# A hybrid encoder in float32: the SwiGLU's first projection cut into column sets of 512 and 384, and its weight sums built up in place

## Chip, cores and metric

The kernel runs on one core of one Trainium2 chip. The metric is the device time of one execution in microseconds (us); of several runs the median counts, and less is better.

## What is computed

Two layers work on an activation x of 512 tokens by 1024 features, all in float32. A layer is a SwiGLU block, a token mixer (pooling, differential attention, a gated linear recurrence, and their merge) and a second SwiGLU block. One RMSNorm ends the program. So there are four SwiGLU blocks, called FFN 1 to FFN 4 here, each with D_FF = 2816:

```python
def swiglu(h, w_in, w_out):
    gate, up = jnp.split(h @ w_in, 2, axis=-1)
    return (jax.nn.silu(gate) * up) @ w_out

    for l in range(DEPTH):
        lam_init = 0.8 - 0.6 * math.exp(-0.3 * l)
        x = x + 0.5 * swiglu(rms_norm(x, ffn1_norm[l]), ffn1_w_in[l], ffn1_w_out[l])
        x = x + token_mixer(rms_norm(x, mix_norm[l]), ...)
        x = x + 0.5 * swiglu(rms_norm(x, ffn2_norm[l]), ffn2_w_in[l], ffn2_w_out[l])
    return rms_norm(x, final_norm)
```

The change touches the four SwiGLU blocks only; the mixer's arithmetic stays.

## The kernel before

**Precision.** TensorE reads float32 in a rounded form, so each operand is split in two. ACT copies a raw weight into the rounded form, `wh<-raw`, and DVE takes the rest, `wl<-raw,wh`. Three matmuls (high by high, high by low, low by high) make one product. The activations are split the same way (`zh`, `zl` for the first projection, `ah`, `al` for the second).

**Seven products.** Both projections of an FFN cut the matrices into 2 by 2 blocks and use seven block products in place of eight (`seven`, L406). In the code's names they are P1 = A11·W00, P2 = A12·W10, Q5 = S1·(W00+W01), Q3 = S4·W11, P6 = S2·(W00+W01+W11), P7 = S3·(W11+W01) and Q4 = A22·(sum of all four). The S are sums of activation blocks. The sums of weights are made in SBUF by transfers: a load (`load_fn`, L362) goes out on SP's queue, and a transfer that adds on landing (`add_fn`, L365) on POOL's queue. P1, Q5, P6 and Q4 share one raw block, `b1`, to which one matrix is added between two products. Q3 and P7 share `b2` if `chain2` is true, which it is for the first projection. In the second, P7 has a block of its own, which it loads and adds to at once:

```python
                if p == "P1":
                    block = b1[n] = Block([ld(0, 0)])
                    acc = ap(0, 1)
...
                elif p == "Q3":
                    block = b2[n] = Block([ld(1, 1)])
                    acc = ap(0, 1) if chain2 else None
                else:
                    block = b2[n] if chain2 else Block([ld(0, 1)], ap(1, 1))
```

**Units.** The work of all four FFNs and both mixers is one list of units. A unit is one weight tile of 128 partitions by up to 1024 elements with its matmuls. In the first projection the 2816 columns of gate and up are cut into sets (`quad`, L460): five of 512 columns, where a product is two units, and one of 256, where all four row chunks of a product fit into one unit. A set is 7 products of 24 matmuls. In the second projection, the output projection, a product has 11 row chunks, thus 66 matmuls in six units, in the order P1, P2, Q5, Q3, P6, P7, Q4. FFN 1 begins with P1; the other three begin their first set with P2 and then P1.

**What sets the order.** The program is written out unit by unit. `loads` (L1387) issues the loads of coming blocks in advance, as long as no more raw blocks are alive than the limit of the unit just finished (`held`: 8 in the first projection, 10 in the second, set at L1440 in `gap`, L1431). `splits_to` (L1424) makes the high parts three units ahead; `split_hi` (L1398) and its `low` (L1412) make the two parts, and behind the low part the block gets its next addition, or is given back and new loads leave. `gap` runs once per unit, and `defer` puts a step some gaps later.

**Pools.** SBUF holds 20 slots of 2 KB per partition (`SLOTS`, L45; for `u`, `v`, `th` and others) and 40 buffers of 4 KB (`BIGS`, L46; for raw blocks, split weights, activations). `two` (L128) gives two halves of one large buffer.

**Around the products.** What a product leaves in PSUM is copied by ACT (`copies` L480, in the second projection L643) or combined by DVE (`c11_` L498, `p6` L534, `q4` L553; `tanh` L493 for the gate). Twice in a set the gated values `v` and `q5` are transposed by TensorE (`transposes` L465, tile `ht`) and copied into `h`. `rsqrt_newton` (L192) and `inv_rms_start` (L199) belong to the norms.

Of the kernel before, what the change touches and what calls it, by code (L numbers as in the profile page):

```python
# [10 lines left out]
AF = mybir.ActivationFunctionType  # L11
# [6 lines left out]
S = 512  # L18
# [23 lines left out]
C_ID, C_ONE, C_DIST, C_EDGE, C_INVW, C_EPS = 0, 128, 256, 256 + 896, 256 + 896 + 32, 256 + 896 + 34  # L42
NCST = C_EPS + 2

SLOTS = 20  # L45
BIGS = 40  # L46
AHEAD = 6.0
LAG = 2
SCFIRST = False
# [57 lines left out]
def trunk_kernel(ctx, tc, xn, pm, fin, cst, bd, f1i, f1o, win, wbp, wba, wbl, wout, f2i, f2o, out):  # L107
# [10 lines left out]
    def slot(dt=F32, name="s"):  # L118
        return sp.tile([128, S], dt, tag="s", name=name)

    def big(dt=F32, name="b"):
        return bp.tile([128, 2 * S], dt, tag="b", name=name)
# [5 lines left out]
    def two(name="t"):  # L128
        return list(pair(F32, name))
# [58 lines left out]
    def defer(n, fn):  # L188

        tasks.setdefault(clock["gap"] + n, []).append(fn)  # L190

    def rsqrt_newton(y0, m):  # L192
        t, r = slot(name="nt"), slot(name="r")
        V.tensor_tensor(out=t, in0=y0, in1=y0, op=MUL)
        V.scalar_tensor_tensor(out=t, in0=t, scalar=-0.5, in1=m, op0=MUL, op1=MUL)
        V.scalar_tensor_tensor(out=r, in0=t, scalar=1.5, in1=y0, op0=ADD, op1=MUL)
        return r

    def inv_rms_start(acc, n, eps, col):  # L199

        ps = bank("nrm")
        PE.matmul(ps, lhsT=ones, rhs=acc, start=True, stop=True)
        y0, m = slot(name="y0"), slot(name="m")
        A.t += 2.6
        A.activation(out=y0, in_=ps, func=AF.Abs_reciprocal_sqrt, scale=1.0 / n, bias=cs[:, C_EPS + col:C_EPS + col + 1])
        V.tensor_scalar(out=m, in0=ps, scalar1=1.0 / n, scalar2=eps, op0=MUL, op1=ADD)
        return y0, m
# [167 lines left out]
    def flat(n=2 * S):  # L375
        return [(0, lambda raw: raw[:, 0:n], 0, (n,))]
# [26 lines left out]

    LEFT = {"P1": "A11", "P2": "A12", "Q5": "S1", "Q3": "S4", "P6": "S2", "P7": "S3", "Q4": "A22"}

    def seven(order, nk, width, left, wap, after, chain2, held, prep=None):  # L406

        upc = 2 * S // width  # L410
        parts = [(k, min(k + upc, nk)) for k in range(0, nk, upc)]
        b1, b2, box = {}, {}, {}
        for p in order:
            name = LEFT[p]
            for n, (k0, k1) in enumerate(parts):
                ld = lambda r, c, k0=k0, k1=k1: load_fn(wap(r, c, k0, k1), k1 - k0, width)
                ap = lambda r, c, k0=k0, k1=k1: add_fn(wap(r, c, k0, k1), k1 - k0, width)
                acc = None
                if p == "P1":
                    block = b1[n] = Block([ld(0, 0)])  # L420
                    acc = ap(0, 1)
                elif p == "Q5":
                    block, acc = b1[n], ap(1, 1)
                elif p == "P6":
                    block, acc = b1[n], ap(1, 0)
                elif p == "Q4":
                    block = b1[n]
                elif p == "P2":
                    block = Block([ld(1, 0)])
                elif p == "Q3":  # L430
                    block = b2[n] = Block([ld(1, 1)])
                    acc = ap(0, 1) if chain2 else None
                else:
                    block = b2[n] if chain2 else Block([ld(0, 1)], ap(1, 1))

                def mm(u, a0, a1, p=p, name=name, k0=k0, k1=k1):
                    if k0 == 0:
                        box[p] = [bank(p), bank(p)]
                    for tt in range(2):
                        acc_ = box[p][tt][:, 0:width]  # L440
                        for k in range(k0, k1):
                            ah, al = (a[:, tt * 128:tt * 128 + 128] for a in left(name, k))
                            wh, wl = (a[:, (k - k0) * width:(k - k0 + 1) * width] for a in (u.hi, u.lo))
                            PE.matmul(acc_, lhsT=ah, rhs=wh, start=k == 0, stop=False)
                            PE.matmul(acc_, lhsT=ah, rhs=wl, start=False, stop=False)
                            PE.matmul(acc_, lhsT=al, rhs=wh, start=False, stop=k == nk - 1)

                def fin(p=p, last=k1 == nk):
                    if last:
                        after[p](box.pop(p))  # L450

                if prep:
                    prep(p, n, len(units))
                units.append(Unit(block, flat((k1 - k0) * width), mm, fin, acc=acc, held=held, nk=k1 - k0))


    def ffn(wi, wo, done, order0):
        H = {}

        def quad(j, order):  # L460
            w = min(S, DFF - j * S)
            u, c11, q5, v, th0, th1 = {}, {}, {}, {}, {}, {}
            held = {}

            def transposes(hh, src):  # L465
                def fn():
                    for kk in range(2):
                        ps = bank("ht")
                        for i in range(w // 256):
                            for tt in range(2):  # L470
                                c = 2 * i + kk
                                PE.transpose(ps[:, i * 256 + tt * 128:i * 256 + tt * 128 + 128], src[tt][:, c * 128:c * 128 + 128], ident)
                        if (hh, kk, j // 2) not in H:
                            H[hh, kk, j // 2] = big(name="h")
                        o = j % 2 * 512
                        defer(1, lambda kk=kk, ps=ps, o=o: A.activation(out=H[hh, kk, j // 2][:, o:o + w], in_=ps[:, 0:w], func=AF.Copy))
                    src.clear()
                return fn

            def copies(dst):  # L480
                def fn(ps):
                    for tt in range(2):
                        dst[tt] = slot(name="u")
                        A.activation(out=dst[tt][:, 0:w], in_=ps[tt][:, 0:w], func=AF.Copy)
                return fn

# [4 lines left out]
                V.scalar_tensor_tensor(out=out_[:, 0:w], in0=a[:, 0:w], scalar=s, in1=b[:, 0:w], op0=op, op1=MUL)  # L491

            def tanh(th, src, t0):  # L493
                for tt in range(2):
                    th[tt] = slot(name="th")
                    A.activation(out=th[tt][:, 0:w], in_=src[tt][:, 0:w], func=AF.Tanh, scale=st["r"][t0 + tt][1])

            def c11_(ps):  # L498
# [27 lines left out]

            def q3(ps):
                def rest():
                    for tt in range(2):
                        v[tt] = slot(name="v")  # L530
                        add(v[tt], ps[tt], q5[tt])
                later.append(rest)

            def p6(ps):  # L534
                def rest():
                    for tt in range(2):
                        add(u[tt], ps[tt], u[tt])
                        add(v[tt], v[tt], u[tt], SUB)
                        mul(v[tt], v[tt], st["r"][tt][2], th0[tt])
                    th0.clear()  # L540

                later.append(rest)
                defer(2, transposes(0, v))

            def p7(ps):
                def rest():
# [6 lines left out]
            def q4(ps):  # L553
                def rest():
                    for tt in range(2):
                        add(u[tt], ps[tt], u[tt])

                def gate():
                    tanh(th1, u, 2)

                    def h1():
                        for tt in range(2):
                            mul(th1[tt], th1[tt], 1.0, u[tt], ADD)
                            mul(q5[tt], q5[tt], st["r"][2 + tt][2], th1[tt])
                        u.clear()
                        th1.clear()
                    later.append(h1)

                later.append(rest)
                defer(1, gate)  # L570
                defer(3, transposes(1, q5))

            def wap(r, c, k0, k1):
                o = c * DFF + j * S
                return wi[r * 512 + k0 * 128:r * 512 + k1 * 128, o:o + w].rearrange("(k p) f -> p k f", p=128)

            seven(order, 4, w, lambda name, k: [a[:, k * 256:k * 256 + 256] for a in zc[name]], wap,
                  {"P1": p1, "P2": p2, "Q5": copies(q5), "Q3": q3, "P6": p6, "P7": p7, "Q4": q4}, True, 8)

        n0 = len(units)  # L580
        later_order = ["P1", "P2", "Q5", "Q3", "P6", "P7", "Q4"]
        for j in range(6):
            quad(j, order0 if j == 0 else later_order)
        nz = len(units) - 1
        add_hook(nz, zc.clear)

# [55 lines left out]

        def copies(dst):  # L643
            def fn(ps):
                for tt in range(2):
                    dst[tt] = slot(name="u")
                    A.activation(out=dst[tt], in_=ps[tt], func=AF.Copy)
            return fn

# [37 lines left out]
        def left(name, k):  # L687
            return [a[:, k % 4 * 256:k % 4 * 256 + 256] for a in comb[name, k // 4]]

        seven(later_order, KF // 2, S, left, wap,  # L690
              {"P1": o_p1, "P2": o_p2, "Q5": o_q5, "Q3": o_q3, "P6": o_p6, "P7": o_p7, "Q4": o_q4}, False, 10, prep)


    def mixer(l, side, done, between):
# [867 lines left out]
```

## Time and profile before

| | |
|---|---|
| runs, us | 2223.81, 2219.13, 2217.24 |
| median, us | 2219.13 |
| profiled execution: its own time, us | 2214.34 |
| its span between first and last record, us | 2212.2 |
| mean granted TensorE clock | 0.985 |
| busy: TensorE (PE), DVE, ACT, POOL | 2106.6 (95%), 1656.1 (75%), 1186.4 (54%), 325.7 us (15%) |
| moved by DMA | 322.98 MB, mean 146 GB/s |

The profile is one execution, recorded in hardware. The table's shares are means over stages with different limits: the output projections move weights fastest, the mixers hardly use POOL's queue. TensorE's records overlap, since matmuls are pipelined, so the time of a stage is read from its window and from the distance between the starts of matmuls, and idle time from the waits. All engine operations carry line 83, the helper that issues them, so tiles tell them apart: `P` and `Q` are PSUM tiles of the products, `raw` a loaded block, `ht` a transpose. L366 is the adding transfer. A clock of 1.00 means the higher of TensorE's two levels all the time.

### The profile page before, as it was taken

Reading aid. Unit: us, or ns where it says so; the run is one execution under the profiler, and the core shown is the slowest. Engines: PE = TensorE matmul, PEld = TensorE weight load, DVE = VectorE, ACT = ScalarE, POOL = GpSimd, SP = SyncE. Lnnn points to the kernel's source line nnn. Section 1 sums busy time; section 2 is a strip of 40 time slices with the busy share of each in tenths; the row PEclk is TensorE's granted clock in tenths of the full one; section 3 lists DMA queues with packets and bytes.
Section 4 is the critical chain, followed back from the end, with each engine's and each line's share of the span. In section 5 each row is a group of like instructions: output and inputs, shape, how many; then the busy total and the mean of one; then the engine's idle time right before and its main releaser. Section 6 shows DMA issues by size and latency. Waiting matters only on the chain.

```text
span 2212.2 us, 25981 instructions
## 1 busy us (share of the span) xinstructions
PE 2106.6 (95%) x9640; PEld 1723.0 (78%) x9640; DVE 1656.1 (75%) x2327; ACT 1186.4 (54%) x1735; POOL 325.7 (15%) x276
## 2 busy tenths in 40 slices
PE   7999898999999999989899999989999999999897
PEld 5888786788787777878777888877887877778786
DVE  6877796598777577769777777966967766777697
ACT  7454464645554554546565545646456535555464
POOL 1122230000000021212212211300000001122131
PEclk9999999999999999999999999999999999999999
DMA  9789697123125287878967878951222344779795
GB/s 250 161 163 194 147 210 202 58 65 98 57 86 156 55 182 178 162 158 198 234 135 153 183 183 181 202 167 47 87 67 67 122 126 97 169 156 188 156 209 129
DMA packets 198030, 322.98 MB, mean 146 GB/s; under 512 B 10384, under 2 KB 72336, under 8 KB 197904
## 3 DMA queue, kind: packets, MB, share of 16 engines
q0 software_dynamic: 76032, 138.43, 36.9%
q1 hardware_dynamic: 121872, 182.90, 25.4%
q8 instruction: 75, 1.23, 0.2%
q14 instruction: 51, 0.42, 0.1%
HBM read 319.19 MB, written 2.10 MB: 145 GB/s over the span
## 4 chain that ended last, share of the span: by engine, by line
PE 52%; DMA 21%; DVE 12%; issue 8%; ACT 6%; POOL 2%; SPq 0%; POOLq 0%; ACTq 0%; DVEq 0%
PE ps L83 17%; PE P L83 11%; DMA raw<-in_f1i_dram 9%; PE Q L83 9%; DMA raw<-in_f2i_dram 7%; DVE wl L83 6%; PE o L83 4%; PE y L83 4%; ACT wh L83 3%; DMA raw<-in_f1o_dram 2%; POOL raw L366 2%; PE v L83 1%; PE sc L83 1%; DMA raw<-in_f2o_dram 1%; PE av L83 1%
## 5 line engine op out<-in xcount | busy, mean ns | idle before, releaser
L83 DVE TENSOR_TENSOR wl<-raw,wh 128x1024 fp32r<-128x1024 f32 (+1 forms) x668 | 705.4, 1076 | 294.3 <-ACT wh L83 291.1
L83 ACT ACTIVATE wh<-raw 128x1024 fp32r<-128x1024 f32 (+1 forms) x668 | 606.5, 936 | 380.8 <-DMA raw<-in_f2i_dram 166.9
L83 PE MATMUL ps<-z,wh 128*128 128x512 f32 x1216 | 380.2, 393 | 0.0
L83 PE MATMUL P<-wl,zh 128*128 128x512 f32 (+1 forms) x768 | 291.8, 380 | 13.0 <-DVE wl L83 12.7
L83 PE MATMUL P<-wh,zh 128*128 128x512 f32 (+1 forms) x768 | 290.6, 378 | 9.6 <-ACT wh L83 9.6
L83 PE MATMUL P<-wh,zl 128*128 128x512 f32 (+1 forms) x768 | 288.5, 376 | 0.0
L366 POOL DMA_DIRECT2D raw<-in_f2i_dram x88 | 107.0, 1232 | 1176.3 <-DVE wl L83 1111.9
L83 PEld LDWEIGHTS ps<-z,wh 128*128 128x128 f32 x1216 | 227.1, 188 | 51.0 <-issue 3.4
L83 PE MATMUL Q<-wl,zh 128*128 128x512 f32 (+1 forms) x576 | 221.1, 384 | 17.0 <-DVE wl L83 17.0
L83 PE MATMUL ps<-z,wl 128*128 128x512 f32 x608 | 237.0, 390 | 0.0
L83 PE MATMUL Q<-wh,zh 128*128 128x512 f32 (+1 forms) x576 | 220.5, 383 | 12.0 <-ACT wh L83 11.8
L83 PE MATMUL Q<-wh,zl 128*128 128x512 f32 (+1 forms) x576 | 217.5, 378 | 0.6 <-DVE zl L83 0.6
L83 PEld LDWEIGHTS P<-wl,zh 128*128 128x128 f32 x768 | 147.4, 192 | 45.7 <-DVE wl L83 21.7
L83 PEld LDWEIGHTS P<-wh,zh 128*128 128x128 f32 x768 | 147.0, 191 | 35.8 <-ACT wh L83 11.0
L366 POOL DMA_DIRECT2D raw<-in_f1i_dram x88 | 107.1, 1236 | 408.9 <-DVE wl L83 336.9
L83 PEld LDWEIGHTS P<-wh,zl 128*128 128x128 f32 x768 | 147.5, 192 | 24.9
L83 PE MATMUL P<-wh,ah 128*128 128x512 f32 x352 | 141.7, 403 | 22.2 <-ACT wh L83 22.2
L83 PEld LDWEIGHTS Q<-wl,zh 128*128 128x128 f32 x576 | 111.5, 194 | 44.2 <-DVE wl L83 26.3
L83 PE MATMUL P<-wl,ah 128*128 128x512 f32 x352 | 141.5, 402 | 4.4 <-DVE wl L83 4.4
L83 PE MATMUL P<-wh,al 128*128 128x512 f32 x352 | 139.8, 397 | 0.0
L83 PEld LDWEIGHTS Q<-wh,zh 128*128 128x128 f32 x576 | 111.4, 193 | 34.4 <-ACT wh L83 15.5
L83 PEld LDWEIGHTS ps<-z,wl 128*128 128x128 f32 x608 | 114.1, 188 | 23.7
(190 smaller groups left out, 3418.7 us busy)
## 6 DMA issues: line engine op xcount, KB each, us to landing
raw<-in_f1i_dram POOLq DMA_DIRECT2D x88, 512.0 KB, 7.4
raw<-in_f2i_dram POOLq DMA_DIRECT2D x88, 512.0 KB, 7.9
raw<-in_win_dram SPq DMA_DIRECT2D x84, 512.0 KB, 4.0
raw<-in_f1i_dram SPq DMA_DIRECT2D x66, 512.0 KB, 7.7
raw<-in_f2i_dram SPq DMA_DIRECT2D x66, 512.0 KB, 5.0
raw<-in_f1o_dram SPq DMA_DIRECT2D x40, 512.0 KB, 7.3
raw<-in_f1o_dram POOLq DMA_DIRECT2D x40, 512.0 KB, 8.6
raw<-in_f2o_dram SPq DMA_DIRECT2D x40, 512.0 KB, 6.6
```

Source lines behind the costliest of these rows:

```text
L83: return fn(*args, **kw)
L366: return lambda raw: GP.dma_start(out=raw[:, 0:n * w].rearrange("p (k f) -> p k f", f=w), in_=src, accum_op=ADD)
```

## The change

Each part in words, with the names of the diff:

- The 2816 columns are cut into four sets of 512 and two of 384. A set of 384 has two units a product, as one of 512; its tiles have 768 elements. There are 84 units in a first projection in place of 77. The tiles `h` are laid out by column chunk (`c0`), so that both widths fit.
- `chain2` is gone: P7 always uses Q3's block, to which its second matrix is added behind Q3's low part.
- `fresh`, true for the first set of FFN 2 to 4: P1's block is not added to, and Q5 loads its own W00 and adds W01.
- `held` is 12, 12, 10, 10, 8, 8 for the six sets, and in the output projection 12 to 14, less at the end.
- `SLOTS` goes from 20 to 14 and `BIGS` from 40 to 43; `u`, `v`, the first `th` and the norms' pairs come from the large pool.
- The transposes of `v` and of `q5` run one gap later (3 and 4 in place of 2 and 3).

```diff
-SLOTS = 20
-BIGS = 40
+SLOTS = 14
+BIGS = 43
...
-        t, r = slot(name="nt"), slot(name="r")
+        t, r = two("nt")
...
-    def seven(order, nk, width, left, wap, after, chain2, held, prep=None):
+    def seven(order, nk, width, left, wap, after, held, prep=None, fresh=False):
...
                 if p == "P1":
                     block = b1[n] = Block([ld(0, 0)])
-                    acc = ap(0, 1)
+                    acc = None if fresh else ap(0, 1)
                 elif p == "Q5":
+                    if fresh:
+                        b1[n] = Block([ld(0, 0)], ap(0, 1))
                     block, acc = b1[n], ap(1, 1)
...
                 elif p == "Q3":
                     block = b2[n] = Block([ld(1, 1)])
-                    acc = ap(0, 1) if chain2 else None
+                    acc = ap(0, 1)
                 else:
-                    block = b2[n] if chain2 else Block([ld(0, 1)], ap(1, 1))
+                    block = b2[n]
...
-        def quad(j, order):
-            w = min(S, DFF - j * S)
+        def quad(j, order, fresh):
+            w = 512 if j < 4 else 384
+            c0 = 4 * j if j < 4 else 16 + 3 * (j - 4)
...
-                        for i in range(w // 256):
+                        cs_ = [c for c in range(w // 128) if (c0 + c) % 2 == kk]
+                        for i, c in enumerate(cs_):
...
             def copies(dst):
                 def fn(ps):
+                    dst.update(enumerate(two("u")))
                     for tt in range(2):
-                        dst[tt] = slot(name="u")
...
-                defer(2, transposes(0, v))
+                defer(3, transposes(0, v))
...
-                defer(3, transposes(1, q5))
+                defer(4, transposes(1, q5))
...
-                o = c * DFF + j * S
+                o = c * DFF + c0 * 128
...
-                  {"P1": p1, "P2": p2, "Q5": copies(q5), "Q3": q3, "P6": p6, "P7": p7, "Q4": q4}, True, 8)
+                  {"P1": p1, "P2": p2, "Q5": copies(q5), "Q3": q3, "P6": p6, "P7": p7, "Q4": q4}, (12, 12, 10, 10, 8, 8)[j], fresh=fresh)
...
-            quad(j, order0 if j == 0 else later_order)
+            quad(j, order0 if j == 0 else later_order, j == 0 and order0[0] == "P2")
...
-              {"P1": o_p1, "P2": o_p2, "Q5": o_q5, "Q3": o_q3, "P6": o_p6, "P7": o_p7, "Q4": o_q4}, False, 10, prep)
+              {"P1": o_p1, "P2": o_p2, "Q5": o_q5, "Q3": o_q3, "P6": o_p6, "P7": o_p7, "Q4": o_q4},
+              dict(P1=12, P2=14, Q5=14, Q3=14, P6=14, P7=12, Q4=9), prep)
```

How the change moves instructions is seen at three places. The first is POOL's queue in the output projection of FFN 1 (`raw_N` are raw blocks by number, `in_f1o` the second projection's weights). Before, from the first addition of P7's own blocks on:

```order
L366 DMA raw_2623<-in_f1o_dram 128x2x512
L366 DMA raw_2648<-in_f1o_dram 128x2x512
L366 DMA raw_2671<-in_f1o_dram 128x2x512
L366 DMA raw_2690<-in_f1o_dram 128x2x512
L366 DMA raw_1640<-in_f1o_dram 128x2x512
L366 DMA raw_1800<-in_f1o_dram 128x2x512
L366 DMA raw_1820<-in_f1o_dram 128x2x512
L366 DMA raw_1844<-in_f1o_dram 128x2x512
L366 DMA raw_1864<-in_f1o_dram 128x2x512
L366 DMA raw_1919<-in_f1o_dram 128x512
L366 DMA raw_2827<-in_f1o_dram 128x2x512
L366 DMA raw_2848<-in_f1o_dram 128x512
```

With the change, from the first addition to Q3's blocks on:

```order
L366 DMA raw_2344<-in_f1o_dram 128x2x512
L366 DMA raw_2364<-in_f1o_dram 128x2x512
L366 DMA raw_2385<-in_f1o_dram 128x2x512
L366 DMA raw_2405<-in_f1o_dram 128x2x512
L366 DMA raw_2407<-in_f1o_dram 128x2x512
L366 DMA raw_2409<-in_f1o_dram 128x512
L366 DMA raw_1824<-in_f1o_dram 128x2x512
L366 DMA raw_1844<-in_f1o_dram 128x2x512
L366 DMA raw_1916<-in_f1o_dram 128x2x512
L366 DMA raw_1944<-in_f1o_dram 128x2x512
L366 DMA raw_2100<-in_f1o_dram 128x2x512
L366 DMA raw_2120<-in_f1o_dram 128x512
```

Before, P7's additions (2623 to 2690, and 2827, 2848) stand on both sides of the six additions for Q4 (1640 to 1919); now the six for P7 go to blocks that Q3 used (2344 to 2409) and stand ahead of a whole row of additions to the blocks of P1 (1824 to 2120).

The second is POOL's queue at the end of the first projection of FFN 1 (`in_f1i`). Before, the last two rows of the fifth set's shared blocks, and the whole set of 256:

```order
L366 DMA raw_1476<-in_f1i_dram 128x2x512
L366 DMA raw_1496<-in_f1i_dram 128x2x512
L366 DMA raw_1192<-in_f1i_dram 128x2x512
L366 DMA raw_1212<-in_f1i_dram 128x2x512
L366 DMA raw_1520<-in_f1i_dram 128x4x256 x2
L366 DMA raw_1612<-in_f1i_dram 128x4x256
L366 DMA raw_1520<-in_f1i_dram 128x4x256
```

With the change, the last set of 384:

```order
L366 DMA raw_1464<-in_f1i_dram 128x2x384
L366 DMA raw_1484<-in_f1i_dram 128x2x384
L366 DMA raw_1464<-in_f1i_dram 128x2x384
L366 DMA raw_1484<-in_f1i_dram 128x2x384
L366 DMA raw_1600<-in_f1i_dram 128x2x384
L366 DMA raw_1800<-in_f1i_dram 128x2x384
L366 DMA raw_1464<-in_f1i_dram 128x2x384
L366 DMA raw_1484<-in_f1i_dram 128x2x384
```

In place of four additions, one after the other to one block or a second one, there are eight, which go to two blocks in turn.

The third is ACT in the first sets of FFN 1, where it copies the transposed values, `h<-ht`, between the splits `wh<-raw` (difference of the two orders, rows that are shifted carry - and +):

```order
 L83 ACTIVATE m<-m 128x8
-L83 ACTIVATE wh<-raw 128x1024 x3
-L83 ACTIVATE h<-ht 128x512 x2
-L83 ACTIVATE wh<-raw 128x1024 x2
+L83 ACTIVATE wh<-raw 128x1024 x4
+L83 ACTIVATE h<-ht 128x512 x2
+L83 ACTIVATE wh<-raw 128x1024
 L83 ACTIVATE th<-u,m 128x512 x2
```

The copies stand one split later, and the `th` behind them as before.

## Rows read from the trace of the kernel before

**Rows 1.** Waits of TensorE: tile, waited for; us in total, times, longest

```profile
PE P L83 <- ACT wh L83: 31.7, 10, 7.2
...
PE ht L83 <- DVE v L83: 5.9, 7, 1.3
```

**Rows 2.** Stages: us, busy PE PEld DVE ACT POOL, clock, DMA share, GB/s

```profile
11.41:68.16 56.75, 47.88 (x195) 37.02 (x194) 43.73 (x76) 41.17 (x66) 9.88 (x9) 0.91 0.87 220
190.49:230.39 39.90, 39.90 (x185) 33.20 (x184) 29.78 (x36) 20.11 (x25) 9.24 (x8) 1.00 0.85 180
230.39:262.00 31.61, 25.70 (x182) 24.41 (x180) 17.38 (x27) 13.99 (x20) 5.15 (x4) 0.89 0.63 122
323.40:338.36 14.96, 14.96 (x68) 12.39 (x66) 13.15 (x14) 6.17 (x7) 5.76 (x5) 1.00 1.12 223
338.36:364.40 26.04, 18.36 (x67) 14.27 (x66) 14.00 (x22) 10.93 (x15) 2.10 (x2) 0.80 1.05 277
752.33:801.51 49.18, 42.76 (x187) 32.77 (x186) 37.63 (x47) 29.28 (x40) 9.66 (x8) 1.00 0.71 150
965.13:996.46 31.33, 24.75 (x182) 23.07 (x180) 17.24 (x26) 13.78 (x20) 5.15 (x4) 0.95 0.65 129
1075.14:1099.88 24.74, 17.89 (x76) 14.11 (x74) 14.62 (x23) 13.46 (x20) 2.10 (x2) 0.86 0.96 246
1325.49:1356.13 30.64, 25.94 (x181) 24.66 (x180) 17.32 (x27) 13.99 (x20) 5.17 (x4) 0.89 0.64 128
1432.64:1457.34 24.70, 17.75 (x67) 13.85 (x66) 13.98 (x22) 10.94 (x15) 2.10 (x2) 0.86 1.05 276
1935.26:1977.41 42.15, 40.66 (x185) 33.06 (x184) 31.04 (x37) 20.95 (x26) 9.70 (x8) 1.00 0.78 161
2058.13:2091.28 33.15, 25.61 (x182) 24.36 (x180) 18.16 (x28) 13.99 (x20) 5.14 (x4) 0.90 0.64 131
2168.02:2188.35 20.33, 17.31 (x67) 13.29 (x66) 15.31 (x24) 12.27 (x17) 2.11 (x2) 0.92 0.79 174
```

**Rows 3.** Timeline of TensorE, set of 256, FFN 1: start, us, operation

```profile
231.11 0.28 PE L83 MATMUL P<-wh,zh 128*128 128x256 f32 x1
...
234.82 0.28 PE L83 MATMUL P<-wl,zh 128*128 128x256 f32 x1
```

**Rows 4.** Timeline of TensorE, FFN 1, product P7 (brackets: idle before)

```profile
356.61 0.80 PE L83 MATMUL P<-wh,ah 128*128 128x512 f32 x1 [7.21 <-ACT wh L83]
...
358.47 0.63 PE L83 MATMUL P<-wh,al 128*128 128x512 f32 x1
358.89 0.63 PE L83 MATMUL P<-wh,ah 128*128 128x512 f32 x1
```

**Rows 5.** Timeline of POOL, output projection of FFN 1

```profile
316.53 1.20 POOL L366 DMA_DIRECT2D raw<-in_f1o_dram  x1 [10.62 <-PE Q L83]
...
339.83 1.20 POOL L366 DMA_DIRECT2D raw<-in_f1o_dram  x1 [7.19 <-DMA raw<-in_f1o_dram]
```

**Rows 6.** Timeline of ACT, set of 256 columns, FFN 2: splits that waited

```profile
972.39 1.06 ACT L83 ACTIVATE wh<-raw 128x1024 fp32r<-128x1024 f32 x1 [8.44 <-DMA raw<-in_f2i_dram]
...
981.89 1.06 ACT L83 ACTIVATE wh<-raw 128x1024 fp32r<-128x1024 f32 x1 [5.73 <-DMA raw<-in_f2i_dram]
...
990.87 1.06 ACT L83 ACTIVATE wh<-raw 128x1024 fp32r<-128x1024 f32 x1 [1.46 <-DMA raw<-in_f2i_dram]
```

**Rows 7.** DMA issues, FFN 2, two stretches: count, KB, us to landing

```profile
raw<-in_f2i_dram POOLq DMA_DIRECT2D x1, 512.0 KB, 5.9
...
raw<-in_f2i_dram POOLq DMA_DIRECT2D x2, 512.0 KB, 12.7
```

**Rows 8.** Groups by form, DVE and ACT: splits, busy us, mean ns, idle before

```profile
L83 DVE TENSOR_TENSOR wl<-raw,wh 128x1024 fp32r<-128x1024 f32 x488 | 589.6, 1221 | 290.1 <-ACT wh L83 287.3 <-PE Q L83 1.7
L83 ACT ACTIVATE wh<-raw 128x1024 fp32r<-128x1024 f32 x488 | 504.5, 1053 | 372.3 <-DMA raw<-in_f2i_dram 166.9 <-DMA raw<-in_f1i_dram 153.6 <-DMA raw<-in_f1o_dram 20.4
```

**Rows 9.** Timeline of ACT, start of FFN 2

```profile
764.01 1.06 ACT L83 ACTIVATE wh<-raw 128x1024 fp32r<-128x1024 f32 x1 [0.93 <-DMA raw<-in_f2i_dram]
```

More of the change, by code (lines that the diff above doesn't have):

```diff
@@ L202, in inv_rms_start @@
         PE.matmul(ps, lhsT=ones, rhs=acc, start=True, stop=True)
-        y0, m = slot(name="y0"), slot(name="m")
+        y0, m = two("y0")
         A.t += 2.6
@@ L453, in seven @@
                     prep(p, n, len(units))
-                units.append(Unit(block, flat((k1 - k0) * width), mm, fin, acc=acc, held=held, nk=k1 - k0))
+                units.append(Unit(block, flat((k1 - k0) * width), mm, fin, acc=acc, held=held[p] if isinstance(held, dict) else held, nk=k1 - k0))
     def ffn(wi, wo, done, order0):
         H = {}
-        def quad(j, order):
-            w = min(S, DFF - j * S)
+        def quad(j, order, fresh):
+            w = 512 if j < 4 else 384
+            c0 = 4 * j if j < 4 else 16 + 3 * (j - 4)
             u, c11, q5, v, th0, th1 = {}, {}, {}, {}, {}, {}
@@ L468, in fn @@
                         ps = bank("ht")
-                        for i in range(w // 256):
+                        cs_ = [c for c in range(w // 128) if (c0 + c) % 2 == kk]
+                        for i, c in enumerate(cs_):
                             for tt in range(2):
-                                c = 2 * i + kk
                                 PE.transpose(ps[:, i * 256 + tt * 128:i * 256 + tt * 128 + 128], src[tt][:, c * 128:c * 128 + 128], ident)
[L473 to L476, printed above, removed]
+                        p0 = (c0 + cs_[0]) // 2
+                        if (hh, kk, p0 // 4) not in H:
+                            H[hh, kk, p0 // 4] = big(name="h")
+                        o, n = p0 % 4 * 256, len(cs_) * 256
+                        defer(1, lambda kk=kk, ps=ps, o=o, n=n, q=p0 // 4: A.activation(out=H[hh, kk, q][:, o:o + n], in_=ps[:, 0:n], func=AF.Copy))
                     src.clear()
@@ L493, in tanh @@
             def tanh(th, src, t0):
+                th.update(enumerate(two("th") if t0 == 0 else (slot(name="th"), slot(name="th"))))
                 for tt in range(2):
-                    th[tt] = slot(name="th")
                     A.activation(out=th[tt][:, 0:w], in_=src[tt][:, 0:w], func=AF.Tanh, scale=st["r"][t0 + tt][1])
@@ L528, in rest @@
                 def rest():
+                    v.update(enumerate(two("v")))
                     for tt in range(2):
-                        v[tt] = slot(name="v")
                         add(v[tt], ps[tt], q5[tt])
@@ L644, in fn @@
             def fn(ps):
+                dst.update(enumerate(two("u")))
                 for tt in range(2):
-                    dst[tt] = slot(name="u")
                     A.activation(out=dst[tt], in_=ps[tt], func=AF.Copy)
```

## The prediction

> **What bounds the kernel now.** I read the waits of TensorE first, then busy times by stage, then the timelines of the engines around the stages that come out too long. TensorE is the engine to watch: what it waits for is above all a split weight, `wh` from ACT, up to 7.2 us at a time, and `v` at the transposes [rows 1]. The stage view tells where this happens [rows 2]. A clean product of the output projection takes 14.96 us for 66 matmuls of 512 columns, 0.2267 us each, and a clean set of 512 columns takes 39.90 us: 168 matmuls are 38.09 us, so its 16 transposes are 1.8 us, 0.113 each. The worst set of 512 that is not the first of its FFN takes 42.15 us. Against these floors two places stand out in each of the four FFNs:
>
> - Product P7 of the output projection takes 26.04, 24.74, 24.70 and 20.33 us in place of 14.96 [rows 2]. Less 0.9 us for eight transposes in the second, that is 35.1 us lost.
> - The set of 256 columns takes 31.61, 31.33, 30.64 and 33.15 us [rows 2]. Its matmuls follow at 0.1197 us (31 steps from 231.11 to 234.82) [rows 3], so 168 of them are 20.1 us, 12 transposes 1.4 us, and the floor is 21.5 us. Lost: 40.7 us.
>
> Set 0 of the later FFNs comes third (49.18 us in the first of the three, 9.3 over 39.9), set 0 of FFN 1 has 56.75 us with a granted clock of 0.91 [rows 2]. The mixers lose little.
>
> **Products P7: the chain of sums.** In the first FFN TensorE stands idle 7.21 us in the middle of P7, and then its matmuls follow at 0.42 us (358.47 to 358.89), so at the lower of the two clock levels, for some microseconds [rows 4]. What was late is a weight: P7 loads its own block and at once adds a second matrix to it, and the adding DMA stands in POOL's queue in order. POOL stood 10.62 us idle ahead of such a DMA, and later 7.19 us more, for the load of P7's last blocks [rows 5]. In the new order no P7 block is loaded: Q3's block gets its addition when Q3's low part is made, 12 units of 2.72 us before P7 needs it, about 30 us, where Q5 and Q4 have always lived with the same distance (product 4 of this projection, P6, takes the clean 14.96 us). The order of POOL shows the six additions alone between those of Q5 and of P6. Price: minus 34 of the 35.1 us; 1 us I leave for restarts. The bound from below is 30 us, if one of the four FFNs keeps a wait as short as the last one's (5.4 us). 22 times 512 KB less are loaded for this; I count nothing for it by itself.
>
> **The narrow sets.** Columns, matmuls and weight loads are the same in number; with a fixed part and a part per column the matmul of 384 columns lies half-way between 0.1197 and 0.2267, 0.173 us, and the sum over both sets is the same as now. The loss comes from the chain P1, Q5, P6, Q4: one block, to which a matrix is added between two products. With 256 columns a product is one unit and the next use comes two units later, 48 matmuls or 5.75 us. The splits on ACT that end these waits begin at 972.39, 981.89 and 990.87 us, 9.5 and 9.0 us apart [rows 6]. So each of three passes is 3.3 to 3.8 us short, and that is the 9.8 us which this set loses. The pass is the addition alone, 5.9 us from issue to landing [rows 7], the two splits, 1.05 and 1.22 us [rows 8], and 1 us between them.
>
> With 384 columns the next use comes four units later, 48 matmuls at 0.173, 8.3 us. The two splits, with 768 elements each, shorten by at most a quarter of their 2.27 us, 0.57; I take 0.5. The addition of 384 KB does not occur before: it is at most the 5.9 us of 512 KB and at least three quarters of it, 4.4; I take 5.2, the middle, since part of the 5.9 does not depend on size. The pass is then 9.2 less 0.5 less 0.7, 8.0 us (7.2 to 8.7), against 8.3: it fits, barely. The page DMA: Bandwidth & Descriptors of the Trainium skill (section Anatomy of one DMA) speaks against small pieces: about 2.0 us fixed and the bytes at 436 GB/s, by which, as an estimate, 384 KB save only 0.3 us; the 3.2 us that it gives for 512 KB do not agree with the 5.9 seen here, and by its difference the pass would be 8.4 us and the whole sum 2 us worse. A set of 512, with 10.9 us between uses, still loses 0 to 2.3 us [rows 2]; with less room I take 2 us for each of the eight sets of 384, 16 us in place of 40.7. Price: minus 25 (from minus 38, nearly nothing lost, to minus 6, over 4 us in each). The 28 more units cost ACT and DVE a fixed start each, at most 0.3 us apiece, and lie beside matmuls: DVE is busy 29.8 of 39.9 us in a set. If DVE were the bound, it would be up to 8 us.
>
> **The start of the later FFNs.** Q5's first two blocks are loaded again, so that they need not wait for P1's split and the addition. What of the wait there was DMA's is 0.93 us at the end of ACT's idle time [rows 9]; the rest is ACT and DVE, busy with the splits of the activations, and stays. Three FFNs: minus 3 us (0 to minus 9, as ACT's later work moves up too). The six additional loads run while the mixer leaves the DMAs idle.
>
> **The transposes.** Those of `v` and `q5` come one unit later. Of TensorE's idle time 5.9 us in 7 waits is `ht` behind DVE's `v` [rows 1], and a restart costs some 0.15 us more. `v` is then long finished; late next is the low part of a weight, since DVE was behind anyway. Minus 5 us (0 to minus 7).
>
> **Pools and prefetch.** The buffers take the same memory. `u`, `v`, `th` and the norm's pairs move to the large pool, which gets three more buffers and up to 14 raw blocks instead of 10. No engine gains work. What changes is when loads leave SP: four more at the start of FFN 1, where additions already run beside loads. An addition there can take what a pair took beside loads elsewhere, 12.7 instead of 5.9 us [rows 7]; set 0 of FFN 1 can thus lose up to 7 us, or gain as much as two, since these loads no longer meet later additions. I take plus 2.
>
> **The sum**: 34 + 25 + 3 + 5 - 2 = 65 us off the profiled execution's 2214.34 us, 2149.3. The median of the three runs shown is 2219.13, 4.8 us above that execution, so I forecast 2154 us for a median.
>
> **Rivals.**
> - The sets of 384 stay bound by their chain. For: a pass of 8.0 us against 8.3 has no room for a load in between, and both pieces of a block queue behind each other. Against: the second piece is also needed a unit later. If every set loses 5 us, it is 40 instead of 16: 2178 us. It decides when a pass takes over 9.5 us. Chance 0.20.
> - The wait in the output projection moves. More raw blocks are alive from Q3 to P7, so a load for P2 or for the mixer could come late. Half of the 34 us back: 2171 us. Against it: POOL's new order has no load to wait for. Chance 0.08.
> - The change does not do what it says, for a matmul of 384 columns, of which there is no row, costs as much as one of 512: 1344 of them by 0.053 us are 72 us, 2226 us, no difference that counts. Against: 256 and 512 columns cost nearly in proportion. Chance 0.03.
> - Slower: the deeper prefetch puts loads beside the additions in all 16 sets of 512. A pass there is 9.2 us of 10.9, 1.7 us of room. If one addition in each set takes 12.7 us instead of 5.9 [rows 7], each set loses 5.1, 82 us in all: 2236 us. It beats the gain from 5.8 us of added latency in a set on. The same page of the Trainium skill (section Queues, rings and completion order) says that each DMA engine takes turns between the queues that have work, and the 12.7 us agree with it. Against: a load leaves only when a block falls free, six in each set, as before; the higher limit adds loads once. Chance 0.05.
>
> **How the numbers follow.** 2154 us has a chance of 0.60; 0.04 is left for still less time. The range takes in all terms at their best (35, 38, 9 and 7 us with nothing lost at the start: 89 us, 2130 us) and at their worst (30 and 6 with plus 7: 29 us, 2190 us), and with these the first two rivals. About 6.7 us, 0.3%, is what a measurement can tell from no change: faster 0.92, same 0.03, slower 0.05.
>
> **What would show it.** P7 at 15 to 16 us in all four FFNs; the two sets of 384 at 31 to 33 us each, where 30.6 is the floor; ACT's splits there ended by DMA but without TensorE idle; no wait of `ht` for `v`; set 0 of FFN 1 no shorter. The forecast is wrong if sets of 512 grow beyond 42 us, if the sets of 384 take 35 or more, or if the output projection shows a new wait for `raw`.

## The result, and the profile after

The changed kernel takes 2159.89 us in the median (four runs, 2157.25 to 2161.17), the kernel before 2221.47: a ratio of 0.9723, interval 0.9702 to 0.9744. That is 61.6 us less; the forecast was 2154, 65 less. The profiled execution took 2160.04 us (span 2158.2, before 2212.2), so 54 us are to be found between the two traces.

Stages after, as in [rows 2] (window, us, busy PE, PEld, DVE, ACT, POOL, clock, DMA share, GB/s): in turn both sets of 384 of FFN 1; set 0, a set of 512, both sets of 384 and P7 of FFN 2; set 0 and the last set of FFN 3; the last set and P7 of FFN 4.

```profile
189.94:221.33 31.39, 30.99 (x184) 30.60 (x182) 24.52 (x36) 17.09 (x26) 8.22 (x8) 1.00 0.82 154
221.33:258.67 37.34, 33.28 (x182) 31.69 (x181) 23.10 (x35) 17.53 (x27) 8.99 (x8) 0.95 0.83 186
739.49:788.78 49.29, 42.31 (x188) 32.81 (x187) 37.38 (x47) 29.12 (x40) 7.29 (x6) 1.00 0.58 126
828.68:868.74 40.06, 40.06 (x185) 33.11 (x184) 32.81 (x39) 21.12 (x27) 11.22 (x10) 1.00 0.75 145
908.64:939.92 31.28, 31.00 (x183) 30.61 (x182) 23.57 (x35) 16.78 (x26) 7.72 (x7) 1.00 0.84 156
939.92:978.24 38.32, 34.03 (x181) 31.76 (x181) 25.51 (x39) 18.77 (x28) 9.66 (x8) 0.96 0.85 195
1055.39:1071.28 15.89, 15.89 (x75) 13.22 (x74) 14.69 (x23) 13.23 (x20) 2.41 (x2) 1.00 0.99 255
1087.13:1136.89 49.76, 43.53 (x186) 33.88 (x184) 38.54 (x48) 27.85 (x38) 8.82 (x8) 0.97 0.62 137
1287.85:1323.78 35.93, 32.42 (x181) 30.25 (x181) 22.93 (x35) 17.39 (x27) 9.01 (x8) 1.00 0.85 190
2004.77:2040.14 35.37, 31.97 (x182) 30.29 (x181) 22.50 (x35) 16.94 (x26) 8.99 (x8) 1.00 0.90 204
2118.99:2134.44 15.45, 15.26 (x67) 12.31 (x66) 15.04 (x24) 12.07 (x17) 0.00 (x0) 1.00 0.37 103
```

- P7 is clean: 14.96, 15.89, 14.96 and 15.45 us in the four FFNs, where it took 26.04 to 20.33 [rows 2]. That is 34.6 us.
- The first set of 384 is nearly clean too, 30.93 to 31.39 us over a floor of 30.6, 2.5 us lost in four. The **last set** is not: 37.34, 38.32, 35.93, 35.37, which is 24.6 lost. Together 27 us in place of the 40.7 of the sets of 256.
- Sets 1 to 3, 512 columns wide, lost 12.4 us in the four FFNs before (over 39.9 for each), and 0.4 now. That gain was not in the forecast at this place. (The expectations of e2, e3 and e5 reckon from slightly lower floors and so give slightly larger losses for the same rows.)
- Set 0 of FFN 2 to 4 takes 148.7 us in all, 3 us more than before (49.18, 46.93 and 49.60).
- The other products of the output projections take 375.9 us in all, before 372.5, so 3.4 more; 2.4 of it are waits for `wl`. The prologue, the work ahead of the first set, takes 2 us more; it shows a granted clock of 0.88 against 1.00 before. e9 below, which differs from the change only in the limit of the last sets, has 1.00 there again, so I do not put it down to the change. Minus 34.6, 14.7 (with 1.1 lost before in the fifth set of 512) and 12.0, plus 3, 3.4 and 2 make minus 53.

TensorE's waits after, as in [rows 1]: `wh` for `P` costs 5.4 us where it cost 31.7, no wait of `ht` is left, and the low part `wl` now leads.

```profile
PE Q L83 <- DVE wl L83: 27.8, 30, 2.2
PE P L83 <- DVE wl L83: 10.9, 15, 1.7
PE P L83 <- ACT wh L83: 5.4, 6, 1.6
```

The two waits for `wl` before, 34.7 us together against 38.7 now:

```profile
PE Q L83 <- DVE wl L83: 17.6, 22, 1.6
PE P L83 <- DVE wl L83: 17.1, 29, 1.2
```

A matmul of 384 columns, from TensorE's timeline in the last set of FFN 2 (26 steps between the two rows, 0.1735 us each, the forecast had 0.173):

```profile
940.99 0.33 PE L83 MATMUL P<-wh,zh 128*128 128x384 f32 x1
...
945.50 0.33 PE L83 MATMUL P<-wh,zl 128*128 128x384 f32 x1
```

### The profile page after: what moved, and what is told of

Its sections match the earlier page's. It is cut to its first block, busy times and chain, and to the rows that moved or that the text cites. A ratio compares the mean times of both kernels' runs of the same rounds, so it can differ in the third digit from the quotient of the medians.

```text
span 2158.2 us, 26082 instructions
## 1 busy us (share of the span) xinstructions
PE 2088.2 (97%) x9640; PEld 1739.0 (81%) x9640; DVE 1660.8 (77%) x2355; ACT 1193.8 (55%) x1763; POOL 344.1 (16%) x292
## 3 DMA queue, kind: packets, MB, share of 16 engines
q0 software_dynamic: 76288, 138.43, 38.5%
q1 hardware_dynamic: 117680, 174.51, 24.6%
## 5 line engine op out<-in xcount | busy, mean ns | idle before, releaser
L83 DVE TENSOR_TENSOR wl<-raw,wh 128x1024 fp32r<-128x1024 f32 (+2 forms) x696 | 708.8, 1040 | 216.5 <-ACT wh L83 214.7
L83 ACT ACTIVATE wh<-raw 128x1024 fp32r<-128x1024 f32 (+2 forms) x696 | 610.0, 906 | 273.2 <-DMA raw<-in_f1i_dram 112.7
L366 POOL DMA_DIRECT2D raw<-in_f2i_dram x96 | 116.2, 1240 | 1142.4 <-DVE gt L83 722.3
L366 POOL DMA_DIRECT2D raw<-in_f1i_dram x96 | 116.4, 1241 | 384.0 <-DVE wl L83 314.8
L83 PEld LDWEIGHTS P<-wl,zh 128*128 128x128 f32 x768 | 145.5, 189 | 30.2 <-DVE wl L83 10.1
L83 PEld LDWEIGHTS P<-wh,zl 128*128 128x128 f32 x768 | 145.5, 189 | 20.1
```

What stands on the lines that cost most here:

```text
L83: return fn(*args, **kw)
L366: return lambda raw: GP.dma_start(out=raw[:, 0:n * w].rearrange("p (k f) -> p k f", f=w), in_=src, accum_op=ADD)
```

## The experiments

Times are medians of four runs (five for the last), each beside the kernel before on the same chip; its medians lay between 2213 and 2221 us, so versions are compared by their ratio, and stages by the profiles. "Lost" is time over the floors: 39.9 us for a set of 512, 30.6 for 384, 21.5 for 256.

**e1: P7's own block.**

```diff
-                    acc = ap(0, 1)
+                    acc = None if own7 else ap(0, 1)
...
-                    block = b2[n]
+                    block = Block([ld(0, 1)], ap(1, 1)) if own7 else b2[n]
```

The output projection sets `own7` and has the limit 10 again, in place of 12 to 14.

> The changed kernel, with P7 of the output projections loading its own block again (24 loads more, limit of raw blocks 10 there). If the chain over Q3's block is what removed the wait (theory): P7 takes 20 to 26 us again in each FFN, about 34 us over the changed kernel, 2194 us. If the wait went because of the new pools or the deeper prefetch (rival): P7 stays under 17 us and the time under 2167.

2191.65 us, ratio 0.9902 (0.9865 to 0.9939). P7 in FFN 1 and FFN 4:

```profile
333.50:358.39 24.89, 18.31 (x67) 14.27 (x66) 14.00 (x22) 10.93 (x15) 0.95 (x2) 0.79 1.01 263
2147.73:2164.85 17.12, 15.86 (x67) 12.23 (x66) 14.12 (x23) 11.30 (x17) 0.70 (x1) 1.00 0.83 183
```

FFN 2 and 3 have 24.50 and 23.52 us. P7 loses 29 us again, so it was not the pools. The run undoes the chain and the higher limit of the output projection together, so it does not tell one from the other. In its FFN 1 the load of P7's last block but one leaves at 321.45 us, 12 us behind the load before it, and the addition to that block, issued at 332.35, lands at 349.46. Whether a higher limit alone would have brought that load in time is not tested.

**e2: five sets of 512 and one of 256, all else as changed.**

```diff
-            w = 512 if j < 4 else 384
-            c0 = 4 * j if j < 4 else 16 + 3 * (j - 4)
+            w = min(S, DFF - j * S)
+            c0 = 4 * j
```

> The changed kernel with the old sets, five of 512 and one of 256 columns. If the loss of the last set is the chain alone, an addition too long for the room between two uses (theory of the forecast): the set of 256 loses 9 to 12 us, 40 in all against 27.6 in the sets of 384 now, so about 2173 us. If it is the loads of the output projection, which run beside the last set's additions whatever its width (rival): it loses 5 to 8 us as the last set of 384 does, and the time is 2157 to 2163.

2164.45 us, 0.9775 (0.9741 to 0.9809). The sets of 256 in FFN 1 and 2 (28.05 and 30.90 in the others):

```profile
230.85:261.80 30.95, 24.18 (x178) 22.89 (x176) 15.22 (x25) 13.24 (x20) 3.96 (x4) 0.94 0.63 119
951.42:979.31 27.89, 24.05 (x177) 22.80 (x176) 14.23 (x23) 12.45 (x19) 3.85 (x3) 0.94 0.68 132
```

They lose 31.8 us, the two sets of 384 lose 27. In these sets the width is worth 5 us, not 25 (the whole span is 8.9 us longer, and the intervals of the two ratios just meet). Both expectations missed, the rival by less.

**e3: transposes one gap earlier.**

```diff
-                defer(3, transposes(0, v))
+                defer(2, transposes(0, v))
```

and the same for `q5`, 3 in place of 4.

> The changed kernel with the transposes one gap earlier, as before. The sets of 512 behind set 0 lost 14.6 us before and 1.1 us now. If only the waits of ht for v were due to this place (forecast): 5 to 7 us come back, 2166 us, and these waits are seen again. If the place of the transposes also causes the waits for the low part at the start of a set (theory now): 9 to 13 us, up to 2172. If pools or prefetch cleared these sets (rival): nothing comes back, 2160.

2158.37 us, 0.9751 (0.9719 to 0.9783): no difference, as the rival had it. TensorE's wait for `v` is back, the waits for `wl` fall from 38.7 to 28.9 us,

```profile
PE Q L83 <- DVE wl L83: 15.0, 21, 1.6
PE P L83 <- DVE wl L83: 13.9, 16, 2.0
PE ht L83 <- DVE v L83: 7.2, 7, 1.3
```

and nothing is lost. What the change put in the place of the wait for `v` is seen at the end of set 0 of FFN 2. First TensorE before, with the longest of these waits:

```profile
794.99 0.98 PE L83 MATMUL ht<-cst,v 128*128 128x128 f32 x7 [1.29 <-DVE v L83]
```

Then the changed kernel: DVE's queue, in which six steps for `v` (the first row is the first of them) stand ahead of the low part of Q4's weight, and TensorE behind it.

```profile
777.00 0.69 DVE L83 TENSOR_TENSOR u<-P,u 128x512 f32<-128x512 f32 x1
...
781.23 1.22 DVE L83 TENSOR_TENSOR wl<-raw,wh 128x1024 fp32r<-128x1024 f32 x1
```

```profile
782.50 0.50 PE L83 MATMUL Q<-wl,zh 128*128 128x512 f32 x1 [2.16 <-DVE wl L83]
```

A wait of 1.3 us for `v` became one of 2.16 us for `wl`, which stands behind `v` in DVE's order.

**e4: no fresh block for Q5.**

```diff
-            quad(j, order0 if j == 0 else later_order, j == 0 and order0[0] == "P2")
+            quad(j, order0 if j == 0 else later_order, False)
```

> The changed kernel with Q5 of the first set of FFN 2 to 4 on P1's block again, six loads fewer. If DVE, not the transfer, ends the waits there (theory now): set 0 takes 49 to 50 us in all three as with the change, time within 2 us of 2160. By the forecast's price, 1 us more each, 2163. If the additional loads get in the way (rival): 46 to 48 us in the third FFN as before, 2157.

2167.13 us, 0.9798 (0.9759 to 0.9837). Set 0 takes 50.41 and 49.08 us in FFN 2 and 3, and in FFN 4

```profile
1806.96:1859.65 52.69, 44.24 (x188) 34.01 (x185) 38.95 (x48) 29.52 (x41) 10.90 (x9) 0.97 0.70 140
```

152.2 us in all against 148.7, that is 1.1, -0.7 and 3.1 us. The ratio is clearly worse than the change's, so the fresh blocks gain something, and my theory that DVE alone ends these waits falls. The size, 3.5 us in three by the trace, fits the forecast's 1 us each but is not shown: the same three sets took 150.5, 145.5 and 147.8 us in e1, e7 and e9, which keep the fresh blocks.

**e5: the limit of raw blocks at 8 in the whole first projection.**

```diff
-... (12, 12, 10, 10, 8, 8)[j], fresh=fresh)
+... 8, fresh=fresh)
```

> The changed kernel with the limit of raw blocks at 8 in all sets of the first projection, as before. The sets of 512 behind set 0 lost 13.2 us (sets 1 to 3) before and 1.1 now, and the place of the transposes gave none of it. If the earlier loads cleared them (theory A): 8 to 12 us come back in sets 1 to 3, about 2170 us. If the pools did (theory B): sets 1 to 3 stay under 3 us in all, 2160 us.

2171.58 us, 0.9793 (0.9773 to 0.9813). Sets 1 to 3 lose 5.5 us again, between the two theories, and the first sets of 384, which have the limit 8 in the changed kernel too, lose 12.2 in place of 2.5 (the last ones 19.5 in place of 24.6). FFN 3's first:

```profile
1263.65:1298.40 34.75, 32.84 (x183) 32.09 (x182) 24.94 (x36) 17.05 (x27) 9.59 (x9) 0.95 0.79 159
```

DMA issues in a set of 512 of FFN 2 (its first 23 us), with the limit of 8 and then with the change (count, KB each, median us to landing):

```profile
raw<-in_f2i_dram POOLq DMA_DIRECT2D x8, 512.0 KB, 8.5
raw<-in_f2i_dram SPq DMA_DIRECT2D x2, 512.0 KB, 7.7
raw<-in_f2i_dram SPq DMA_DIRECT2D x1, 384.0 KB, 9.3
```

```profile
raw<-in_f2i_dram POOLq DMA_DIRECT2D x8, 512.0 KB, 6.5
raw<-in_f2i_dram SPq DMA_DIRECT2D x1, 384.0 KB, 9.4
```

With the lower limit three loads leave while the set's eight additions run, and an addition takes 8.5 us in the median; with the higher limit one load is left there, and an addition takes 6.5. It is so in all four FFNs: in the set at this place the first load leaves 15 us after the set's start with the limit of 8, and 22.7 with the change; the others have left before.

**e6: the old pools, new limits.** `SLOTS` 20, `BIGS` 40, and `u`, `v`, `th` and the norms' pairs in small buffers.

> The changed kernel with the old pools (20 small, 40 large, u, v, th and the norms in small ones) and the new limits. Theory A (earlier loads): sets 1 to 3 stay under 3 us in all, though loads may wait for a large buffer, 2158 to 2165 us. Theory B (pools): sets 1 to 3 lose 8 to 12 us again, about 2170 us.

2171.99 us, 0.9794 (0.9771 to 0.9816). Sets 1 to 3 lose 2.6 us, the first sets of 384 5.5, and the last sets 33 in place of 24.6, FFN 3's for one:

```profile
1296.82:1335.56 38.74, 34.06 (x182) 31.77 (x182) 27.15 (x40) 18.91 (x28) 9.87 (x9) 0.96 0.86 200
```

Neither theory had this: sets 1 to 3 came out as A had it, the time as B had it. The pools earn as much as the limits by the medians (12 us each), but in other sets.

**e7: a limit of 6 in the last set.**

```diff
-... (12, 12, 10, 10, 8, 8)[j], fresh=fresh)
+... (12, 12, 10, 10, 8, 6)[j], fresh=fresh)
```

> The changed kernel with a limit of 6 raw blocks in the last set only, so that the output projection's first loads leave later. If these loads slow the last set's additions (theory): the additions to Q4's and P7's blocks land in 5 to 7 us in place of 10 to 12, the last sets lose under 2 us each in place of 5 to 8, about 18 us in all, and P1 of the output projection loses some of it, 0 to 4 us each: 2142 to 2158. If the chain or DVE's work bounds the last set by itself (rival): it loses 5 to 8 us as now, and P1 more: 2162 or more.

2150.81 us, 0.9698 (0.9676 to 0.9721). The last sets lose 18.9 us, 3.9 to 5.6 each, where the theory had under 2. The late additions still took 10 to 12 us: in FFN 2 three loads leave beside them, 15 to 21 us into the set. The time came out as the theory had it, the loss and the additions did not, and the interval meets the change's.

**e8: the sets of 384 in places 2 and 3** (`w = 384 if j in (2, 3) else 512`, chunks from 0, 4, 8, 11, 14, 18; copies of `h` cut where they cross a tile).

> The changed kernel with the two sets of 384 in places 2 and 3, so that the last set has 512 columns. If the last set loses by the loads that run beside it, the room of 10.9 in place of 8.3 us between two uses cuts the loss by 2 to 3 us in each FFN, and the sets of 384 in the middle stay under 1 us: 2148 to 2156. If the width of the set decides by itself (rival): both sets of 384 lose 5 to 8 us, 2175 us or more.

2147.48 us, 0.9690 (0.9665 to 0.9714). FFN 2, the second set of 384 and the last set, now of 512:

```profile
859.00:894.09 35.09, 31.56 (x181) 30.29 (x181) 24.85 (x38) 17.22 (x26) 9.66 (x8) 1.00 0.84 168
934.15:974.05 39.90, 39.90 (x185) 33.19 (x184) 31.14 (x36) 22.71 (x30) 8.38 (x8) 1.00 0.91 211
```

The last set is clean though nine loads leave in it as before; it has 10.9 us between two uses. But the first narrow sets lose 6.7 us in the four FFNs and the second ones 16.7, away from the output projection's loads, so both expectations missed. Neither those loads nor the place at the end is the cause by itself; it points to the next set's loads, whichever they are, in a set with little room.

The two narrow sets together lose 23.4 us in place of 27. Most of what the span gains, 11.6 us, is elsewhere: set 0 of FFN 2 to 4 takes 139.8 us in place of 148.7, FFN 2's for one:

```profile
739.18:786.24 47.06, 41.88 (x187) 32.88 (x186) 36.88 (x46) 29.03 (x40) 7.29 (x6) 1.00 0.55 115
```

e11 below has 140.0 there too, e12 147.0. Why is open.

**e9: a limit of 4 in the last set** (as e7, 4 for 6).

> The changed kernel with a limit of 4 raw blocks in the last set: the output projection's loads can leave only when the set's own blocks are given back. If the loads beside the additions make the last set's loss (theory): additions in the last set land in 5 to 8 us, it loses under 2.5 us in each FFN, and P1 of the output projection loses 3 to 8 us instead, since its blocks come late; 2148 to 2165. If the chain is too long for 8.3 us even alone (rival): the last sets still lose 4 us or more each, and P1 more: over 2165.

2147.08 us, 0.9694 (0.9669 to 0.9718). The last sets of FFN 1 and 2 (35.15 and 32.59 in FFN 3 and 4):

```profile
218.97:251.85 32.88, 31.03 (x182) 30.34 (x181) 25.49 (x38) 18.29 (x28) 9.66 (x8) 1.00 0.80 150
933.89:966.39 32.50, 31.00 (x181) 30.36 (x181) 22.94 (x35) 17.41 (x27) 8.97 (x8) 1.00 0.79 153
```

Lost: 10.7 us in place of 24.6; FFN 3's 4.55 us is over the 2.5 that the theory allowed. DMA issues in some 20 us from about the start of a narrow set of FFN 2: with the change in the first one, in the last one, and in the last one of e9:

```profile
raw<-in_f2i_dram POOLq DMA_DIRECT2D x8, 384.0 KB, 6.6
raw<-in_f2i_dram SPq DMA_DIRECT2D x1, 384.0 KB, 3.3
```

```profile
raw<-in_f2i_dram POOLq DMA_DIRECT2D x8, 384.0 KB, 8.1
raw<-in_f2o_dram SPq DMA_DIRECT2D x4, 512.0 KB, 8.3
raw<-in_f2o_dram SPq DMA_DIRECT2D x1, 256.0 KB, 6.8
```

```profile
raw<-in_f2i_dram POOLq DMA_DIRECT2D x8, 384.0 KB, 6.5
raw<-in_f2o_dram SPq DMA_DIRECT2D x1, 512.0 KB, 8.7
```

In the median an addition takes 6.6 us with one load issued there, 8.1 with five, 6.5 with one again; the last two additions of e9's set, which run beside that load, still take 9.9 and 10.3. P1 of the output projections lost only 1.3 us in all for its late loads, not 3 to 8.

**e10: old pools and the limit of 8 together.**

> The changed kernel with both the old pools and the limit of 8; each alone cost 12 us. If the pools matter because they make room for the earlier loads (theory): the two together cost about as much as one alone, 2170 to 2176 us. If they are two separate effects (rival): they add up, 2182 to 2187.

2187.47 us, 0.9871 (0.9845 to 0.9898). The two add up, my theory falls. Sets 1 to 3 lose 10.7 us, nearly the 12.4 of the kernel before. Both sets of 384 of FFN 3:

```profile
1274.24:1308.91 34.67, 32.96 (x183) 32.06 (x182) 24.90 (x36) 17.08 (x26) 9.39 (x8) 0.95 0.80 155
1308.91:1345.79 36.88, 33.24 (x182) 31.91 (x181) 23.39 (x36) 18.13 (x27) 8.72 (x8) 0.95 0.88 199
```

Over the four FFNs these two sets lose 43.7 us. The kernel before lost 40.7 in the sets of 256 and about 1 in the sets of 512 ahead of them: with the old pools and the old limit of the first projection, the width gains **nothing**.

**e11: as e8, with limits 8 and 6 in the narrow sets.**

> The kernel with the sets of 384 in places 2 and 3, limits 8 and 6 in these two sets. The second of them lost 4.4 us on average at a limit of 10. If the next set's loads beside its additions make this loss (theory): under 2 us each, its additions in 5 to 8 us, and at most 1 us more in the set behind it; 2137 to 2146 us. If a narrow set behind a narrow one loses by itself (rival): 4 us or more each, 2147 us or later loads on top.

2145.72 us, 0.9690 (0.9658 to 0.9722). The second narrow sets lose 9.6 us in place of e8's 16.7, the first 3.7 in place of 6.7, but the sets of 512 behind give 5.9 of these 10.1 us back (42.13 us in FFN 2's set 4, 42.01 in FFN 3's set 5). Half confirmed: the loss falls, though not under 2 us each, and loads held back seem to meet the next additions.

**e12: the sets of 384 apart, in places 1 and 3, limit 8.**

> The changed kernel with its sets of 384 apart, in places 1 and 3, each between sets of 512, limit 8 in both. Side by side, the first narrow set lost about 1 us at limit 8 and the second 2.6 to 6. If it is the place behind another narrow set that costs (theory): 0.5 to 1.5 us in each of the eight, 4 to 12 us in all, 2138 to 2146 us. If any narrow set whose next loads are 512 KB loses (rival): 3 to 4.5 us in each, 2148 to 2158 us.

2153.09 us, 0.9715 (0.9699 to 0.9732). FFN 2's two narrow sets:

```profile
782.63:815.29 32.66, 30.99 (x184) 30.60 (x183) 25.06 (x37) 17.76 (x26) 9.66 (x8) 1.00 0.77 134
855.23:886.81 31.58, 31.02 (x184) 30.63 (x182) 24.24 (x36) 17.82 (x27) 9.50 (x8) 1.00 0.83 164
```

All eight lose 10.9 us, 1.0 to 2.1 each, about as the theory had it. The profiled execution took 2143.29 us and is the fastest of the five; their median is where the rival had it. In the time this version is not told from the changed kernel.

## Why the prediction was right, and where it was not

The sign, the size and the range hold, but as a sum whose terms were partly wrong and made up for each other. That they did was luck: the narrow sets and the transposes gave some 15 us less than forecast, and sets 1 to 3 gave 12 us that the forecast had not put there. One of its own signs of being wrong came true as well: the last sets of 384 take 35.37 to 38.32 us, where 35 or more was to count against it.

- **P7, minus 34**: right in place and size. 34.6 us in the trace, and e1 gives 29 of it back. That P7's own block, loaded late, was the wait is borne out; that the chain alone removed it, without the higher limit that came with it, is not shown.
- **The narrow sets, minus 25**: this step failed. The claim was that a pass of 8.0 us fits into 8.3. The parts were right: 0.1735 us a matmul, and the shortest additions of 384 KB take 5.2 to 5.4 us. But with loads beside it, an addition takes 8.1 in the median of FFN 2's last set and up to 13.1 in FFN 1's, and the pass no longer fits. Additions run beside each other too, and that is not enough: of the 64 of 384 KB in the changed kernel, 13 had at most 0.5 us of a load beside them and took 5.2 to 7.3 us, median 6.1; the other 51 took up to 13.1, median 7.4. Width alone is worth 5 us in these sets (e2), and nothing under the old pools and limit (e10): 14.7 us were gained where 25 were forecast, 27 lost where 16 were allowed. The second rival, a new wait for loads in the output projection, did not come; that stage lost 3.4 us by other waits, in place of 17. The first, that the chain stays the bound, came half true: 27 us lost, between the 16 of the forecast and its 40. An addition of 384 KB is shorter than one of 512 KB (6.0 us) by 0.6 to 0.8 us; by the Trainium skill (DMA: Bandwidth & Descriptors, section Anatomy of one DMA) it would be 0.3, so the trace differs here.
- **Pools and prefetch, plus 2**: this step failed by its sign. I saw the two sides, that earlier loads can meet additions and that they no longer meet later ones, but in the sum looked for both in set 0 of FFN 1 alone and gave the second at most 2 us. Set 0 of FFN 1 hardly changed (56.67 us after, 56.75 before). The second side ruled in the other sets: fewer loads are left to run beside their additions (e5). Undone, the limits cost 12.3 us of the span (e5), the pools 16.8 (e6), both 29.8 (e10); by the medians 12, 12 and 28. Of the 29.8, 17 are in the sets of 384 and 10 in sets 1 to 3. The slower rival, deeper prefetch against the additions in the sets of 512, is thereby refuted: they went from 40 to 42 us down to 39.9.
- **The transposes, minus 5**: failed. The wait for `v` went, but I named what is late next, the low part, and then counted nothing for it. It costs about as much (e3).
- **The later FFNs' start, minus 3**: the sign is right by e4's time; the size, 3.5 us by its trace, lies within what these sets vary by. Set 0 nevertheless grew by 3 us in all, of it 3 in FFN 3 (46.93 to 49.76 us). e3 has 46.78 there, but e7 and e9, whose transposes are as in the change, have 47.63 and 47.90, so the growth is not put down to the transposes; its cause is open.

The undone parts sum to 31 + 9 + 5 - 1 + 30 = 74 us by the spans of e1, e2, e4, e3 and e10, more than the 54 that the spans differ by: so the parts overlap. Why the pools matter is not settled. In each of the four last sets ten loads leave with the old pools (e6) and nine with the change, so part of it may be the same effect.

What makes the loss of the last sets is shown by e9: with fewer loads beside the additions they lose 10.7 us in place of 24.6, and nothing else was changed. That room matters as well is borne out by e8's last sets, which are clean at a width of 512; its two narrow sets lost nearly as much as before in their new place. With the narrow sets apart they lost 10.9 in place of 27 (e12), but there five and four loads leave in them, where it was four and nine, so the place is not shown apart from the loads. The best ratios, 0.9690 to 0.9698 (e7, e8, e9, e11), are below the change's 0.9723, but the intervals overlap; a better version is likely, not shown.

## What to carry over

A transfer that another step waits for must be priced at its length beside what else is in flight, not alone: here 5.4 us became 8 to 13, and the room between two uses was 8.3. When buffers and look-ahead change together with the work's shape, ask when each load leaves and what it then runs beside; undone, buffers and look-ahead cost 29.8 us of the span, the shape 8.9. And when a wait is moved away, price the next one in the same engine's queue.

## What was not expected of the hardware

The packets of an adding transfer take twice as long for their bytes as those of a plain load. The page after (queue, packets, MB, share of 16 engines' time; the first is POOL's, the second holds SP's):

```profile
q0 software_dynamic: 76288, 138.43, 38.5%
q1 hardware_dynamic: 117680, 174.51, 24.6%
```

38.5% for 138.43 MB is 0.278% a MB, 24.6% for 174.51 MB is 0.141. How much of this is waiting for each other no run tells. The Trainium skill (DMA: Bandwidth & Descriptors, section Queues, rings and completion order) says that an engine takes turns between queues with work; 6.6 us with one load and 8.1 with five agree with it.
